# Where z enters the first branch, when the second branch is scaled, and how the forget rows are cleared

## The chip, the cores and the metric

The kernel runs on one core of one Trainium2 chip, as one launch. The metric is the device time of one execution in microseconds. A core has five engines that run their own instruction queues: TensorE (PE in the profile; its weight loads are shown as PEld), VectorE (DVE), ScalarE (ACT), GpSimd (POOL) and SyncE (SP), which here only issues transfers. Each engine runs its instructions in the order in which the program has them, and an instruction that waits holds all that stand behind it on its engine.

## The reference, cut to what matters

The block has two attention branches over the same normalised input, 512 tokens, 8 heads of 64 in each. The first ("fox", f) adds a forget term to its logits, the second ("moba", m) has rotated queries and keys and no forget term. Each branch's result is multiplied by a gate path made from z:

```
h = rms_norm(x, norm_g)
fq, fk, fv, fz, mq, mk, mv, mz, ga, gb, fl = split(h @ w_in)
c = cumsum(log_sigmoid(fl + b_f))
logits = q k^T * scale + c[query] - c[key]          # first branch, causal
y_fox = softmax(logits) @ v  * silu(fz)
y_moba = moba_attention(rope(q), rope(k), v) * silu(mz)
merged = sigmoid(ga + b0) * (y_fox @ w_fox) + sigmoid(gb + b1) * (y_moba @ w_moba)
out = x + merged @ w_out
```

## The kernel before, in words

Matrix products run as three products of a high and a low part each (`wh_`/`wl_`, `Gh`/`Gl`, `yh`/`yl`), which ACT and DVE make. Weights come in blocks of 512 KB, issued by SP into four buffers (`wr`).

Attention goes by four groups of four heads: first branch a and b, second branch a and b (`attn_group`, called from the loop over `plan`). A group has two pairs of heads. `Tr(pr)` transposes the pair's queries and keys on TensorE, and ACT and DVE make from them `QS`, `KH` and the low key part `KL`; half of `KH` is copied to the other 64 partitions by a transfer on ACT's queue. `Aa(h)` makes a head's logits (lines 558 and 559) and exponentials. `Bb(h)` transposes these, multiplies them by v and writes the head's half of the pair's tile y (line 638). `Yp(pr)` scales y by the inverse sums of the exponentials. Those go out through DRAM and come back spread over the partitions into the tile `rinv_bc` (`sums_out`, `sums_in`), which has one buffer in all but the last pair of the kernel; y of the first branch (`ypair`) has one buffer too.

In the first branch `Yp` also brings in z's gate `ZS` (lines 650 and 651): POOL multiplies it into the inverse sums, DVE multiplies y by that, and `gated` splits y into the two parts that the later product with `w_fox` reads. In the second branch `Yp` is one product on POOL (line 654); its gate comes later (line 806) and its split after that (`gated`, lines 508 and 509).

The four tiles `KLt[o][pr]` hold `KL` in 64 of their rows and, in the first branch, four forget rows in the other 64, brought in by SP (line 544); the remaining rows are zero from the start (`zero_kl`). The second branch uses the same tiles and needs the forget rows zero: `moba_begin` does this with four memsets of 32 rows on POOL, after the last logits of the first branch that read each tile. It is called between the second and third group.

POOL also does the powers, the scaling and the rotation of the queries and keys (lines 333, 335 and 365 to 371).

The program is written group by group, with projections of the next group laid between the parts (`inter`). The order on each engine is not the written one: the context is created with `schedule_with_timeline_sim=True`, a planner that simulates durations and orders each engine's instructions from that, by written order where several are ready. `attn_group` returns four lists: the head, the body, the tail, and the steps that go into the next group's body behind its first logits (`gate` in the loop).

Of the kernel before, what the change touches and what calls it, by code (L numbers as in the profile page):

```python
# [7 lines left out]
F32 = mybir.dt.float32  # L8
F32R = mybir.dt.float32r
AF = mybir.ActivationFunctionType  # L10
OP = mybir.AluOpType
# [18 lines left out]
def fox_moba_kernel(ctx: ExitStack, tc, xT, x, w_in, w_fl, w_fox, w_moba, w_out, cst, rope, out):  # L30


    nc = tc.nc
    V, A, G, T = nc.vector, nc.scalar, nc.gpsimd, nc.tensor
# [14 lines left out]
    def t2(tag, bufs, name, shape=(P, 512), dt=F32):  # L49
        pool = stage["pool"] if tag in ("qs", "pt", "pc", "ys") else sb  # L50
        return pool.tile(list(shape), dt, name=name, tag=tag, bufs=bufs)

    def pst(tag, bufs, name):
        return ps.tile([P, 512], F32, name=name, tag=tag, bufs=bufs)
# [4 lines left out]
    def tp(name):  # L59
        return pst("tp", 3, name)  # L60
# [347 lines left out]
    ZS = {}  # L408
# [81 lines left out]
    def moba_begin():  # L490
        for o in range(2):
            rows = slice(HD, HD + 32) if o == 0 else slice(0, 32)
            for tl in KLt[o]:
                G.memset(tl[rows, :].bitcast(F32), 0.0)


    Y = {}
# [7 lines left out]
    def gated(br, gp, y):  # L505
        yh = t2("y", 13, f"yh{br}{gp}", dt=F32R)
        yl = t2("y", 13, f"yl{br}{gp}", dt=F32R)
        A.activation(yh, y, AF.Copy)
        V.tensor_tensor(out=yl, in0=y, in1=yh.bitcast(F32), op=OP.subtract)
        Y[br, gp] = (yh, yl)  # L510

    def attn_group(br, half, gq, gk):
        fox = br == "f"
# [4 lines left out]
        def Tr(pr):  # L518
            def go():
                pq, pk = tp("p_qT"), tp("p_kT")  # L520
                for t in range(NT):
                    T.transpose(pq[:, t * P:(t + 1) * P], qn[:, t, pr * P:(pr + 1) * P], ident)  # L522
                for t in range(NT):
                    T.transpose(pk[:, t * P:(t + 1) * P], kn[:, t, pr * P:(pr + 1) * P], ident)
                for o in range(2):
                    h = 2 * pr + o
                    me, ot = (slice(0, HD), slice(HD, P)) if o == 0 else (slice(HD, P), slice(0, HD))
                    qs = t2("qs", 4, "QS", dt=F32R)
                    kh = t2("qs", 4, "KH", dt=F32R)
                    kl = KLt[o][pr]  # L530
                    A.activation(qs[me, :], pq[me, :], AF.Copy, scale=gq[me, :])  # L531
                    V.scalar_tensor_tensor(qs[ot, :], pq[me, :], gq[me, :], qs[me, :].bitcast(F32),  # L532
                                           op0=OP.mult, op1=OP.subtract)
                    A.activation(kh[me, :], pk[me, :], AF.Copy, scale=gk[me, :])
                    nc.scalar.dma_start(out=kh[ot, :].bitcast(F32), in_=kh[me, :].bitcast(F32))
                    V.scalar_tensor_tensor(kl[me, :], pk[me, :], gk[me, :], kh[me, :].bitcast(F32),
                                           op0=OP.mult, op1=OP.subtract)
                    q2 = qs
                    if fox:
                        q2 = Q2t[o]  # L540
                        lr = slice(HD, HD + 4) if o == 0 else slice(0, 4)
                        hh = hb + h
                        nc.sync.dma_start(out=q2[lr, :].bitcast(F32), in_=LR[hh:32:8, :].bitcast(F32))
                        nc.sync.dma_start(out=kl[lr, :].bitcast(F32), in_=LR[32 + hh:64:8, :].bitcast(F32))
                        nc.scalar.dma_start(out=q2[me, :].bitcast(F32), in_=qs[me, :].bitcast(F32))
                    st[h] = (qs, kh, kl, q2)
            return go

        def Aa(h):
            def go():  # L550
                qs, kh, kl, q2 = st[h]
                hh = hb + h
                pts = []
                for i in range(NT):
                    n = P * (i + 1)
                    lg = pst("lg", 2, "lg")
                    qt = slice(i * P, (i + 1) * P)
                    T.matmul(lg[:, :n], qs[:, qt], kh[:, :n], start=True, stop=False)  # L558
                    T.matmul(lg[:, :n], q2[:, qt], kl[:, :n], start=False, stop=True)  # L559
                    pt = stage["pool"].tile([P, n], F32, name=f"p{i}", tag=f"p{i}", bufs=2)  # L560
                    V.tensor_tensor_reduce(pt, lg[:, :n], mask[:, 512 - n:512], -0.125, 3.0e38,  # L561
                                           op0=OP.add, op1=OP.min, accum_out=mkn[:, hh, i:i + 1])
                    A.activation(pt, pt, AF.Exp, bias=mkn[:, hh, i:i + 1], scale=-1.0,  # L563
                                 accum_out=rs[:, hh, i:i + 1])
                    pts.append(pt)
                st[h] = pts
                if h % 2:
                    inverse_sums(h // 2)
                elif h:
                    sums_in(0)  # L570
            return go
# [4 lines left out]
        def inverse_sums(pr):  # L576
            h0 = hb + 2 * pr
            V.reciprocal(ri[:, h0:h0 + 2, :], rs[:, h0:h0 + 2, :])
# [16 lines left out]
        def Bb(h):  # L595
            def go():
                pts, vt = st[h], VT[f"{br}v{half}"]
                o = h % 2
                pv = pst("pv", 1, "pv")

                def blk(dst, i, j):
                    T.transpose(dst, pts[i][:, j * P:(j + 1) * P], ident)

                def spl(p, n):
                    tag, w, bufs = ("pt", 512, 4) if n == 512 else ("pc", 256, 2)
                    hi = t2(tag, bufs, "pth", (P, w), F32R)
                    lo = t2(tag, bufs, "ptl", (P, w), F32R)
                    A.activation(hi[:, :n], p[:, :n], AF.Copy)
                    V.tensor_tensor(out=lo[:, :n], in0=p[:, :n], in1=hi[:, :n].bitcast(F32), op=OP.subtract)
                    return hi, lo  # L610
                def pvm(j, hl, c0, n, start, stop):
                    T.matmul(pv[:, P * j:P * j + n], vt[:, j, h, :], hl[0][:, c0:c0 + n], start=start, stop=False)  # L612
                    T.matmul(pv[:, P * j:P * j + n], vt[:, j, h, :], hl[1][:, c0:c0 + n], start=False, stop=stop)  # L613
                pa = tp("p_a")
                for i in range(4):
                    blk(pa[:, i * P:(i + 1) * P], i, 0)
                pb = tp("p_b")
                for i in range(1, 4):
                    blk(pb[:, (i - 1) * P:i * P], i, 1)
                blk(pb[:, 384:512], 3, 3)  # L620
                ha = spl(pa, 512)
                hbb = spl(pb, 512)
                pc = tp("p_cc")
                for i in range(2, 4):
                    blk(pc[:, (i - 2) * P:(i - 1) * P], i, 2)
                hc = spl(pc, 256)
                pvm(0, ha, 0, 512, True, False)
                pvm(1, hbb, 0, 384, False, False)
                pvm(3, hbb, 384, 128, False, False)
                pvm(2, hc, 0, 256, False, True)  # L630
                pr = h // 2
                if o == 0:
                    st["y", pr] = t2("ys", 1, "ypair") if fox else t2("y", 13, f"ym{half}{pr}")
                y = st["y", pr]
                me, ot = (slice(0, HD), slice(HD, P)) if o == 0 else (slice(HD, P), slice(0, HD))
                sh = t2("uy", 1, "ysh")
                A.activation(sh[me, :], pv[ot, :], AF.Copy)
                V.tensor_tensor(out=y[me, :], in0=pv[me, :], in1=sh[me, :], op=OP.add)
                if o == 0:
                    sums_out(pr)  # L640
                elif pr:
                    sums_in(1)
            return go

        def Yp(pr):
            def go():
                y, rb = st["y", pr], st["r", pr]
                gp = 2 * (half == "b") + pr
                if fox:
                    G.tensor_tensor(out=rb, in0=ZS[br, gp], in1=rb, op=OP.mult)  # L650
                    V.tensor_tensor(out=y, in0=y, in1=rb, op=OP.mult)
                    gated(br, gp, y)
                else:
                    G.tensor_tensor(out=y, in0=y, in1=rb, op=OP.mult)
                    YM[gp] = y
            return go


        return ([Tr(0)], [Aa(0), Aa(1), Tr(1), Bb(0), Aa(2), Bb(1), Yp(0), Aa(3)], [Bb(2), Bb(3)], [Yp(1)])


    FS, MG = {}, {}
# [725 lines left out]
```

## Time and profile before

| | |
|---|---|
| median of 3 runs | 423.7 us (423.02 to 425.86) |
| profiled execution | 423.75 us |
| its span | 422.0 us |
| TensorE busy | 414.9 us |
| VectorE busy | 333.2 us |
| ScalarE busy | 273.6 us |
| GpSimd busy | 107.0 us |

The span is the time from the first to the last instruction of the profiled execution; the device time has 1.75 us more around it. Busy time counts an engine's instructions, not the waits and the issuing of transfers. The second branch's logits begin at about 167 us and the products with `w_fox` at about 247 us. The shares are means over the whole span; the stretches differ.

### The profile page before, as it was taken

How to read it: one execution, taken by the hardware profiler on the slowest of the kernel's cores; microseconds unless marked ns; L12 is line 12 of the kernel's file. 1: busy time of each engine (PE TensorE's matmuls, PEld its weight loads, DVE VectorE, ACT ScalarE, POOL GpSimd, SP SyncE). 2: the span in 40 equal slices, each digit the busy share in tenths (PEclk: the TensorE clock that was granted, in tenths of full speed). 3: DMA queues.
4: the chain of work that ended last, by engine and by line, in shares of the span. 5: the costliest groups of instructions: out<-in, count | busy, mean ns of one | idle time of the engine just before them, and what ended most of it. 6: DMA issues, size and time to landing. Idle time of an engine off the chain costs nothing.

```text
span 422.0 us, 7872 instructions
## 1 busy us (share of the span) xinstructions
PE 414.9 (98%) x2956; PEld 388.1 (92%) x2956; DVE 333.2 (79%) x571; ACT 273.6 (65%) x521; POOL 107.0 (25%) x127
## 2 busy tenths in 40 slices
PE   7999999999999999999999999999999999999996
PEld 6998899999999999999999998899999989988884
DVE  5669978797878997596977997637989675788982
ACT  4975437878769866796568876446847525685550
POOL 1049300252114690317600125120000020022240
PEclk9999999999999999999999999999999999999999
DMA  7981144654263662231048736623141726796394
GB/s 236 400 324 51 56 144 124 189 171 155 50 210 80 223 193 73 78 110 43 0 127 239 266 120 222 244 99 110 37 164 53 247 51 151 238 247 112 84 163 155
DMA packets 29703, 63.73 MB, mean 151 GB/s; under 512 B 3424, under 2 KB 10272, under 8 KB 29664
## 3 DMA queue, kind: packets, MB, share of 16 engines
q1 hardware_dynamic: 16880, 42.57, 30.3%
q0 software_dynamic: 3968, 9.44, 10.3%
q10 hardware_dynamic: 8816, 11.21, 9.1%
q8 instruction: 23, 0.38, 0.4%
q14 instruction: 16, 0.13, 0.1%
HBM read 52.56 MB, written 6.32 MB: 140 GB/s over the span
## 4 chain that ended last, share of the span: by engine, by line
PE 82%; DMA 6%; DVE 6%; ACT 2%; issue 1%; POOL 1%; SPq 1%; DVEq 0%; ACTq 0%
PE pb_GA L907 3%; PE pb_GB L907 3%; PE pb_GA L906 3%; PE pb_GB L904 3%; PE pb_GA L904 3%; PE pb_GB L906 3%; PE po L1093 3%; PE po L1091 3%; PE po L1092 3%; PE lg L559 2%; PE lg L558 2%; PE pv L613 2%; PE pv L612 2%; PE pGZ0a L771 2%; PE pGZ0b L771 2%; DMA x<-in_x_dram 2%
## 5 line engine op out<-in xcount | busy, mean ns | idle before, releaser
L333 POOL TENSOR_TENSOR ff<-ss,mh 128x8 f32<-128x8 f32 x16 | 27.8, 1741 | 60.6 <-DVE ss L331 51.8
L563 ACT ACTIVATE p<-p,negm 128x128 f32<-128x128 f32 (+1 forms) x64 | 35.7, 558 | 8.7 <-DVE negm L561 8.3
L561 DVE CUSTOM_DVE_ANT_0 p<-lg,mask 128x128 f32<-128x128 f32 (+1 forms) x64 | 30.2, 484 | 8.5 <-PE lg L559 8.2
L134 ACT ACTIVATE wh_GB<-wr_gb 128x1024 fp32r<-128x1024 f32 x14 | 14.6, 1058 | 13.4 <-PE pm L670 5.9
L136 DVE TENSOR_TENSOR wl_GA<-wr_ga,wh_GA 128x1024 fp32r<-128x1024 f32 x14 | 17.6, 1266 | 6.2 <-ACT wh_GA L134 6.2
L558 PE MATMUL lg<-KH,QS 128*128 128x128 f32 (+1 forms) x64 | 21.0, 333 | 0.2 <-DMA KH<-KH 0.2
L1053 ACT ACTIVATE wh_o<-wr_o 128x1024 fp32r<-128x1024 f32 x14 | 14.8, 1058 | 9.7 <-PE pb_GB L906 2.8
L974 POOL DMA_DIRECT2D uGB<-f x4 | 3.5, 869 | 69.4 <-issue 59.4
L136 DVE TENSOR_TENSOR wl_GB<-wr_gb,wh_GB 128x1024 fp32r<-128x1024 f32 x14 | 16.8, 1220 | 5.0 <-ACT wh_GB L134 5.0
L134 ACT ACTIVATE wh_GA<-wr_ga 128x1024 fp32r<-128x1024 f32 x14 | 14.6, 1059 | 9.2 <-PE pb_GA L906 5.9
L1054 DVE TENSOR_TENSOR wl_o<-wr_o,wh_o 128x1024 fp32r<-128x1024 f32 x14 | 16.9, 1218 | 2.4 <-ACT wh_o L1053 2.4
L532 DVE SCALAR_TENSOR_TENSOR QS<-p_qT,cs,QS 64x512 fp32r<-64x512 f32 x16 | 12.0, 750 | 4.1 <-ACT QS L531 3.7
L531 ACT ACTIVATE QS<-p_qT,cs 64x512 fp32r<-64x512 f32 x16 | 10.9, 680 | 4.1 <-PE p_qT L522 2.8
L904 PE MATMUL pb_GB<-Gh,wh_GB 128*128 128x256 f32 x48 | 13.5, 281 | 0.0
L904 PE MATMUL pb_GA<-Gh,wh_GA 128*128 128x256 f32 x48 | 13.5, 281 | 0.0
L906 PE MATMUL pb_GB<-Gl,wh_GB 128*128 128x256 f32 x48 | 13.5, 281 | 0.0
L906 PE MATMUL pb_GA<-Gl,wh_GA 128*128 128x256 f32 x48 | 13.5, 281 | 0.0
L907 PE MATMUL pb_GB<-Gh,wl_GB 128*128 128x256 f32 x48 | 13.5, 281 | 0.0
L907 PE MATMUL pb_GA<-Gh,wl_GA 128*128 128x256 f32 x48 | 13.5, 281 | 0.0
L669 PE MATMUL pf<-yhf,wh_wf 128*128 128x512 f32 x32 | 12.9, 402 | 0.0
L670 PE MATMUL pf<-ylf,wh_wf 128*128 128x512 f32 x32 | 12.7, 396 | 0.0
L558 PEld LDWEIGHTS lg<-KH,QS 128*128 128x128 f32 x64 | 12.1, 189 | 0.6 <-issue 0.3
(479 smaller groups left out, 1820.0 us busy)
## 6 DMA issues: line engine op xcount, KB each, us to landing
wr_ga<-in_w_in_dram SPq DMA_DIRECT2D x8, 512.0 KB
wr_gb<-in_w_in_dram SPq DMA_DIRECT2D x8, 512.0 KB
wr_o<-in_w_out_dram SPq DMA_DIRECT2D x8, 512.0 KB
xt<-in_xT_dram SPq DMA_DIRECT2D x8, 256.0 KB
x<-in_x_dram SPq DMA_DIRECT2D x8, 256.0 KB
KH<-KH ACTq DMA_DIRECT2D x16, 128.0 KB
s_dramh<-sum_h ACTq DMA_DIRECT2D x8, 256.0 KB
s_draml<-xt ACTq DMA_DIRECT2D x8, 256.0 KB
```

Of the source, the lines that this page charges most:

```text
L134: A.activation(hi[:, :, 0:n], src, AF.Copy)
L136: eng.tensor_tensor(out=lo[:, q, 0:n], in0=src[:, q], in1=hi[:, q, 0:n].bitcast(F32), op=OP.subtract)
L333: G.tensor_tensor(out=f2, in0=ss.rearrange("p t h -> p (t h)"), in1=mh, op=OP.pow)
L558: T.matmul(lg[:, :n], qs[:, qt], kh[:, :n], start=True, stop=False)
L561: V.tensor_tensor_reduce(pt, lg[:, :n], mask[:, 512 - n:512], -0.125, 3.0e38, op0=OP.add, op1=OP.min, accum_out=mkn[:, hh, i:i + 1])
L563: A.activation(pt, pt, AF.Exp, bias=mkn[:, hh, i:i + 1], scale=-1.0, accum_out=rs[:, hh, i:i + 1])
L771: T.matmul(o, x, y, start=(new and h == 0 and k == 0 and i == 0), stop=(k == 3 and i == 2), skip_group_check=True)
L904: T.matmul(o, hi[:, k, cc], lh, start=(n < 3 and c == 0 and k == 0), stop=False, skip_group_check=True)
L906: T.matmul(o, hi[:, k, cc], ll, start=False, stop=False, skip_group_check=True)
L907: T.matmul(o, lo[:, k, cc], lh, start=False, stop=(k == 3), skip_group_check=True)
L1053: A.activation(wide(hi), wide(R[key, c]), AF.Copy)
L1054: V.tensor_tensor(out=wide(lo), in0=wide(R[key, c]), in1=wide(hi).bitcast(F32), op=OP.subtract)
```

## The change

Three edits. In the first branch POOL multiplies z's gate into y itself, and DVE then multiplies by the inverse sums. In the first group of the second branch the first scaling, `Yp(0)`, goes from before the group's last logits into the late list, so that both scalings are written in the next group's body. And the forget rows are cleared by four transfers on SP, which copy four zero rows of the same tile over them, in place of four memsets on POOL.

```diff
     def moba_begin():
         for o in range(2):
             rows = slice(HD, HD + 32) if o == 0 else slice(0, 32)
+            a = rows.start
             for tl in KLt[o]:
-                G.memset(tl[rows, :].bitcast(F32), 0.0)
+                nc.sync.dma_start(out=tl[a:a + 4, :].bitcast(F32), in_=tl[a + 4:a + 8, :].bitcast(F32))
...
                 if fox:
-                    G.tensor_tensor(out=rb, in0=ZS[br, gp], in1=rb, op=OP.mult)
+                    G.tensor_tensor(out=y, in0=y, in1=ZS[br, gp], op=OP.mult)
                     V.tensor_tensor(out=y, in0=y, in1=rb, op=OP.mult)
                     gated(br, gp, y)
...
-        return ([Tr(0)], [Aa(0), Aa(1), Tr(1), Bb(0), Aa(2), Bb(1), Yp(0), Aa(3)], [Bb(2), Bb(3)], [Yp(1)])
+        early, late = ([Yp(0)], [Yp(1)]) if fox or half == "b" else ([], [Yp(0), Yp(1)])
+        return ([Tr(0)], [Aa(0), Aa(1), Tr(1), Bb(0), Aa(2), Bb(1)] + early + [Aa(3)], [Bb(2), Bb(3)], late)
```

## Rows read from the trace of the kernel before

**Rows 1.** The page, busy us (share of the span) and instructions of each engine.

```profile
PE 414.9 (98%) x2956; PEld 388.1 (92%) x2956; DVE 333.2 (79%) x571; ACT 273.6 (65%) x521; POOL 107.0 (25%) x127
```

**Rows 2.** Busy time by stretch: from:to, length, engines, granted clock, transfers' share.

```profile
core 0: us, PE busy (x) PEld busy (x) DVE busy (x) ACT busy (x) POOL busy (x), PEclk, DMA share, GB/s
...
141.00:160.00 19.00, 18.66 (x152) 18.14 (x151) 16.86 (x34) 13.06 (x30) 17.31 (x21) 1.00 0.58 183
```

**Rows 3.** TensorE's waits, 60 to 280 us: total us, times, longest.

```profile
PE p_qT L522 <- POOL qn_mqa L371: 0.3, 1, 0.3
PE lg L558 <- DMA KH<-KH: 0.2, 1, 0.2
```

**Rows 4.** Timeline of TensorE: start us, us, line, operation, tiles, [idle before].

```profile
153.12 0.29 PE L305 MATMUL pj_mva<-wh_mva,Gh 128*128 128x256 f32 x1
153.24 0.28 PE L306 MATMUL pj_mva<-wl_mva,Gh 128*128 128x256 f32 x1
153.87 0.44 PE L522 MATMUL p_qT<-ident,qn_mqa 128*128 128x128 f32 x2 [0.34 <-POOL qn_mqa L371]
...
160.57 0.38 PE L522 MATMUL p_qT<-ident,qn_mqa 128*128 128x128 f32 x2
...
166.92 0.28 PE L559 MATMUL lg<-KL,QS 128*128 128x128 f32 x1
```

**Rows 5.** The chain that ended last, between 143 and 160: start us, us, what.

```profile
147.60 1.30 POOL rinv_bc L650
...
153.36 0.46 POOL qn_mqa L371
```

**Rows 6.** Timeline of POOL, columns as in rows 4; last row by line 494.

```profile
121.44 0.52 POOL L494 MEMSET KL<- 32x512 f32 x1 [14.65 <-issue]
...
144.42 0.52 POOL L494 MEMSET KL<- 32x512 f32 x1
...
154.38 1.65 POOL L333 TENSOR_TENSOR ff<-ss,mh 128x8 f32<-128x8 f32 x1
...
158.66 0.46 POOL L371 TENSOR_TENSOR qn_mqa<-ra,rb 128x128 f32<-128x128 f32 x1
...
202.50 2.33 POOL L654 TENSOR_TENSOR yma<-yma,rinv_bc 128x512 f32<-128x512 f32 x1 [3.88 <-DVE yma L638]
...
L494 POOL MEMSET KL<- x4: 514/518/520, 121.4 to 153.8; 32x512 f32 x4
```

**Rows 7.** Timeline of DVE, 147 to 165 us.

```profile
147.61 2.38 DVE L136 TENSOR_TENSOR wl_mkb<-wr_mkb,wh_mkb 128x1024 fp32r<-128x1024 f32 x1 [0.50 <-ACT wh_mkb L134]
...
153.03 0.69 DVE L638 TENSOR_TENSOR ypair<-pv,ysh 64x512 f32<-64x512 f32 x1
...
155.42 0.69 DVE L651 TENSOR_TENSOR ypair<-ypair,rinv_bc 128x512 f32<-128x512 f32 x1
...
164.68 1.23 DVE L136 TENSOR_TENSOR wl_mqb<-wr_mqb,wh_mqb 128x1024 fp32r<-128x1024 f32 x1
```

**Rows 8.** Tile KL (ns: min/median/max), SP's and ACT's timelines, the chain's first load.

```profile
L544 SPq DMA_DIRECT2D KL<-LR x8: 577/577/607, 68.7 to 102.5; - x8
...
135.65 1.57 SPq L210 DMA_DIRECT2D wr_mqb<-in_w_in_dram  x2
...
163.58 1.06 ACT L134 ACTIVATE wh_mqb<-wr_mqb 128x1024 fp32r<-128x1024 f32 x1
...
8.94 7.00 DMA wr_fka<-in_w_in_dram
```

**Rows 9.** The chain at 214 us, and TensorE's row that follows it.

```profile
214.66 4.17 DMA KH<-KH
...
218.97 0.30 PE L558 MATMUL lg<-KH,QS 128*128 128x128 f32 x1 [0.17 <-DMA KH<-KH]
```

**Rows 10.** First reader of the first branch's y; split of the second's (tile yma).

```profile
247.26 0.39 PE L669 MATMUL pf<-yhf,wh_wf 128*128 128x512 f32 x1
...
L508 ACT ACTIVATE yhm<-yma x2: 628/630/632, 275.4 to 302.6; 128x512 fp32r<-128x512 f32 x2
```

## The prediction, made before the change was run

> **What bounds the kernel now.** I read the page's busy shares first: TensorE (PE) is busy for 98% of the span, VectorE (DVE) for 79%, ScalarE (ACT) for 65%, GpSimd (POOL) for 25% [rows 1]. So a change to POOL's work is worth only what it takes from, or adds to, TensorE's pauses. The view of busy time by stretch says where POOL is nevertheless tight: between 141 and 160 us it works 17.31 of 19.00 us, and that is also a stretch in which TensorE falls short, by 0.34 us, at full granted clock [rows 2]. Third, TensorE's waits between 60 and 280 us, the whole part in which changed instructions run: there are two, 0.3 us for POOL's rotated queries `qn_mqa` (line 371) and 0.2 us for a copy of key halves, `KH` [rows 3].
>
> The busy bar hides a part of a pause, because the end of a matmul is modelled. Starts are better: 153.12 to 153.24 is the usual 0.12 us for 256 columns, and then the next matmul, the transpose of `qn_mqa`, starts at 153.87, 0.63 us later [rows 4]. So this wait costs 0.63 - 0.12 = 0.51 us. The chain of waits shows what stood before that transpose: POOL's z product from 147.60 to 148.90, four rotation and scaling steps, and the last of them at 153.36 [rows 5]. The z product (line 650) has nothing to do with the transpose; it merely stands ahead in POOL's queue. The second wait starts from a `KH` copy of 4.17 us and shows 0.17 us idle [rows 9].
>
> **Part 1, z is multiplied into y.** No instruction is added or removed: four POOL products of 128x512, each with two full operands, stay four, and so do the four DVE products. Old: POOL waits for the inverse sums, new: for y, the pair's weighted values (line 638). In the second group of the first branch the second half of y starts at 153.03 for some 0.69 us, so is there at 153.72, while the old product ran at 147.60 [rows 5, 7]. It can therefore not run ahead of the first `qn_mqa` chain any more: 1.30 us leave that chain, against 0.51 us of wait. Gain: 0.51 us if the transposes keep their place in TensorE's order, 0 if the planner moves them up with their inputs and meets the same slow POOL steps again. I take 0.51, as the row at hand has 1.30 us to give and the memset below 0.52 more.
>
> What is late next: the product now wants POOL at 153.72, and POOL starts the second `qn_mqa` chain at 154.38, ending at 158.66 + 0.46 = 159.12; TensorE transposes that half at 160.57, so there are 1.45 us of room for a product of 1.30 [rows 4, 6]. It fits, barely. On DVE the scaling of y stood at 155.42 [rows 7]; it now waits for POOL, and behind it in DVE's queue stand the evacuations of the value projection. That is the slow case below. The results, the first branch's products split into two parts, are first read by TensorE at 247.26 [rows 10]: lateness of the values themselves costs nothing.
>
> **Part 2, forget rows.** Removed from POOL: four memsets, 0.518 us each in the median, 2.07 us together, of which one (144.42) lies in the chain that TensorE waits for, and one only held POOL with nothing else to do (14.65 us before 121.44) [rows 6]. On the chain that is part of the 0.51 already counted, so nothing is added. New on SyncE's queue (SP): four transfers of four rows. The nearest issue is the transfer of the forget rows themselves, the same four rows of the same tile: 0.577 us on SP [rows 8], so 4 x 0.577 = 2.3 us of SP. Its landing has no row; bounds are near nothing and the 4.17 us of a `KH` copy inside SBUF [rows 9], which is 16 times as many rows, and I take the upper one. The last memset began at 153.8 [rows 6]; a transfer from there would land by 158.0, and the second branch first multiplies with such a tile at 166.92 [rows 4]: 8.9 us of cover. If that cover were gone, each late clear would cost up to its 4.17 us.
>
> Behind a clear that must wait, SP holds weight loads. Worst order: the last tile's clear ahead of the load of `wr_mqb`, issued at 135.65. The clear waits for the last forget product, no later than 153.8; the load (7.00 us for a like one in the chain) would land near 161.4 with the 0.577 us of the clear, and its split starts at 163.58 [rows 6, 8]. So even this costs nothing, with 2.2 us left. Price 0, bounds 0 and 2.3 us (all four issues uncovered).
>
> **Part 3, the second branch's first scaling later.** The product at 202.50 (2.33 us, after 3.88 us in which POOL was held for y) leaves its place [rows 6]. The inverse sums have one buffer there, so the load for the next pair waits for it; the split of these values starts only at 275.4 [rows 10], so I price it at 0. It could free the `KH` wait, 0.17 us [rows 9]; but that chain starts from TensorE's own transposes, so I take 0. Bounds: 0.17 us gained to nothing.
>
> **Sum.** 423.75 us, the profiled execution (span 422.0, so 1.75 us around it), - 0.51 + 0 + 0 = 423.24. The median of the three runs is 423.7, 0.05 below the profiled one, so I forecast 423.2. Run to run the kernel moved from 423.02 to 425.86.
>
> **A rule weighed.** At 147.61 DVE's split of `wr_mkb`, two operands in SBUF, took 2.38 us; the same shape at 164.68 took 1.23 [rows 7]. POOL's z product ran at the same moment [rows 5]. So one overlap cost DVE 1.15 us. The Trainium skill, SBUF — State Buffer, section SBUF: two separate sides, says that GpSimd shares a port pair with VectorE as a lock, and that a VectorE instruction with two SBUF inputs fully blocks until GpSimd's reading instruction is over. The trace agrees with that here; by the rule the four products could block DVE for up to 4 x 1.30 = 5.2 us (an estimate from that page and the row), and the sum would lie that much nearer the slow case. I leave DVE's loss at one overlap, as now, since the number of products stays four.
>
> **Rivals.**
>
> *The wait is kept* (0.27). The program's order on each engine comes from a planner that simulates durations; the memset that held POOL 14.65 us shows that it misjudges them [rows 6]. It may move the transposes up as soon as it thinks the inputs are there. Then a 0.5 us wait stands there again: 423.7, 423.2 to 424.2.
>
> *DVE is held for POOL: slower* (0.20). Place: 153.7 to 160.4. If POOL runs the product after the second `qn_mqa` chain, it ends at 159.12 + 1.30 = 160.42, and DVE, standing at its scaling since 155.42, is held 5.0 us [rows 6, 7]. TensorE fills a projection unit of 24 matmuls in 24 x 0.12 = 2.9 us [rows 4], and the projections have two accumulator buffers, so it can hide about one unit: 5.0 - 2.9 = 2.1 us lost, 423.7 + 2.1 = 425.8. With the lock of the rows above on top (1.15) it is 427.0. It decides as soon as DVE's hold passes 2.9 us. Against it: the planner knows of POOL's queue and would put DVE's scaling later.
>
> *SP's clears are in the way* (0.05): 423.7 + 2.3 = 426.0.
>
> *The lock decides* (0.04), the page's rule as a mechanism of this kernel: three more overlaps of 1.15 us on DVE, 3.45 us, in stretches where TensorE waits for DVE: 423.7 + 3.45 = 427.2, and over 1% slower with any wait beside it.
>
> *The change moves nothing it names*: that the order on all engines stays but for the swapped operands is part of the second case.
>
> **How the numbers follow.** Forecast 0.42 (422.6 to 423.8), wait kept 0.27, DVE held 0.20, SP 0.05, lock 0.04, and 0.02 for a gain that I can't see. Below, both waits and nothing new would give 423.7 - 0.51 - 0.17 = 423.0; with the 0.7 us by which the fastest run lies below the median, 422.3, and I set 422.1. Above, DVE held is 425.8, and I set 426.2, which leaves the lock and the worse half of DVE held outside. What a measurement of this kernel can tell from no change is 1%, 4.2 us: below 419.5 or above 427.9. TensorE's waits in the changed part sum to 0.68 us, so faster than that is next to excluded: 0.02. Slower takes DVE held at its worst and the lock: 0.06. Within: 0.92.
>
> **What would show it.** Right: no TensorE wait for `qn_mqa`, POOL's z product behind y at each of four places, POOL under 17 us busy between 141 and 160, memsets gone, and SP's clears well before the second branch's first logits. Wrong: a TensorE pause of over 1 us between 150 and 170 that goes back to DVE's scaling and from there to POOL; or DVE steps of 2 us beside the z products; or a weight split that waits for a load behind a clear. A pause anywhere that traces to none of these would mean that the new plan itself, not the three edits, decides.

## The result: slower by 1.1%, by a change of order in a stage that no edit touches

| | before | after |
|---|---|---|
| median | 423.64 us (422.99 to 425.86, 6 runs) | 428.64 us (426.69 to 430.54, 6 runs) |
| ratio after to before | | 1.0112, interval 1.0075 to 1.0149 |
| profiled execution, span | 423.75 us, 422.0 us | 426.69 us, 424.9 us |

The forecast was 423.2 us within 422.1 to 426.2. The time lies outside of it, on the side that had a chance of 0.06. The profiled execution is the shortest of the six, so its trace holds 2.9 us of the 5.0 by which the medians differ; the rest is looked for in three more traces below.

The page of the changed kernel, the row that answers to [rows 1]:

```profile
PE 415.3 (98%) x2956; PEld 388.4 (91%) x2956; DVE 330.0 (78%) x571; ACT 272.9 (64%) x521; POOL 105.1 (25%) x123
```

Every engine but TensorE has less to do, DVE by 3.2 us. So nothing became costlier by its busy time; the loss must be in waits. TensorE's waits from 60 to 420 us, in total, number and longest:

```profile
PE pb_GB L906 <- ACT wh_GB L134: 1.9, 1, 1.9
PE lg L559 <- DMA KH<-KH: 0.9, 2, 0.6
```

Beside [rows 3], the wait for `qn_mqa` is gone, the one for `KH` has grown, and there is a new one of 1.9 us in a stage that no edit touches: the gates (`GA`, `GB`), whose first matmuls stood at 277 us before. TensorE's timeline shows the places (start, us, line, operation, tiles, idle before):

```profile
153.01 0.39 PE L560 MATMUL lg<-KL,Q 128*128 128x512 f32 x1
153.24 0.38 PE L523 MATMUL p_qT<-ident,qn_mqa 128*128 128x128 f32 x2
...
218.14 0.28 PE L613 MATMUL pv<-pth,v_mva 128*128 128x256 f32 x1
219.01 0.30 PE L559 MATMUL lg<-KH,QS 128*128 128x128 f32 x1 [0.59 <-DMA KH<-KH]
...
309.04 0.28 PE L908 MATMUL pb_GA<-Gl,wh_GA 128*128 128x256 f32 x1
311.20 0.39 PE L906 MATMUL pb_GB<-Gh,wh_GB 128*128 128x256 f32 x1 [1.89 <-ACT wh_GB L134]
311.43 0.28 PE L908 MATMUL pb_GB<-Gl,wh_GB 128*128 128x256 f32 x1
311.54 0.28 PE L909 MATMUL pb_GA<-Gh,wl_GA 128*128 128x256 f32 x1
```

At 153 the transposes of `qn_mqa` follow without a gap, where [rows 4] had 0.63 us between two starts. At 218 there are 0.87 us between starts, at 309 there are 2.16. Two matmuls of `GB` stand there in the middle of a unit of `GA`: 19 more of that unit follow them, from 311.54 to 313.68. In the kernel before, the same two matmuls of `GB` stand between two units of `GA`:

```profile
311.19 0.28 PE L904 MATMUL pb_GB<-Gh,wh_GB 128*128 128x256 f32 x1
311.31 0.28 PE L906 MATMUL pb_GB<-Gl,wh_GB 128*128 128x256 f32 x1
311.43 0.28 PE L904 MATMUL pb_GA<-S3h,wh_GA 128*128 128x256 f32 x1
```

Counted in the traces, 48 matmuls of `GA` come behind them before and 70 in the changed kernel. So the planner also moved these two up in TensorE's order, by 22 matmuls or 22 x 0.12 = 2.6 us.

The chain of waits goes back from that pause (start, us, what):

```profile
304.93 1.23 DVE wl_GA L136
306.18 3.81 DMA wr_gb<-in_w_in_dram
...
310.09 1.07 ACT wh_GB L134
...
311.20 0.39 PE pb_GB L906
```

DVE's low part of a weight block frees the buffer, SP issues the load of the next block (`wr_gb`), it lands 3.8 us later, ACT splits it, TensorE starts. In the kernel before that load was issued earlier, by SP's timeline of before:

```profile
303.56 0.33 SPq L871 DMA_DIRECT2D wr_gb<-in_w_in_dram  x1
```

That left room there. ACT's timeline of before has the split of that block:

```profile
308.41 1.06 ACT L134 ACTIVATE wh_GB<-wr_gb 128x1024 fp32r<-128x1024 f32 x1 [1.23 <-PE pb_GA L906]
```

The high part is ready at 309.47 there, and TensorE reads it at 311.19. The load is 2.6 us later now, because DVE is. DVE's timeline of the kernel before, in the stretch where that begins:

```profile
291.95 0.68 DVE L917 TENSOR_TENSOR uGA<-pb_GA,e_GA 128x512 f32<-128x512 f32 x1
292.55 1.21 DVE L866 TENSOR_TENSOR wr_ga<-wr_ga,wr_ga 128x1024 f32<-128x1024 f32 x1
294.59 0.69 DVE L917 TENSOR_TENSOR uGA<-pb_GA,e_GA 128x512 f32<-128x512 f32 x1 [0.82 <-PE pb_GA L907]
295.37 1.22 DVE L953 TENSOR_TENSOR f<-uGA,f 128x1024 f32<-128x1024 f32 x1
```

And of the changed kernel (the first three rows are of the edited stage, used further down):

```profile
148.70 1.22 DVE L136 TENSOR_TENSOR wl_mkb<-wr_mkb,wh_mkb 128x1024 fp32r<-128x1024 f32 x1
...
152.56 0.69 DVE L639 TENSOR_TENSOR ypair<-pv,ysh 64x512 f32<-64x512 f32 x1
...
154.66 0.69 DVE L652 TENSOR_TENSOR ypair<-ypair,rinv_bc 128x512 f32<-128x512 f32 x1
...
292.28 0.68 DVE L919 TENSOR_TENSOR uGA<-pb_GA,e_GA 128x512 f32<-128x512 f32 x1
294.91 0.69 DVE L919 TENSOR_TENSOR uGA<-pb_GA,e_GA 128x512 f32<-128x512 f32 x1 [1.95 <-PE pb_GA L909]
295.70 1.23 DVE L955 TENSOR_TENSOR f<-uGA,f 128x1024 f32<-128x1024 f32 x1
296.85 1.22 DVE L868 TENSOR_TENSOR wr_ga<-wr_ga,wr_ga 128x1024 f32<-128x1024 f32 x1
299.25 2.36 DVE L136 TENSOR_TENSOR wl_GA<-wr_ga,wh_GA 128x1024 fp32r<-128x1024 f32 x2 [1.19 <-ACT wh_GA L134]
```

Before, the second weight subtraction (L866) stood ahead of the sum (L917) that must wait for TensorE, and filled that wait: 0.82 us idle. Now it stands behind the sum and behind a product: DVE idles 1.95 us, and then 1.19 us more for ACT's split. That split needs the late subtraction, which ends at 298.07, and it also stands behind an exponential on ACT that waits for TensorE and ends at 298.10; before, it stood ahead of that exponential. Either would have held it. ACT's row in the changed kernel:

```profile
297.50 0.60 ACT L916 ACTIVATE e_GA<-pb_GA 128x512 f32<-128x512 f32 x1 [0.95 <-PE pb_GA L909]
```

From 299.25 to 312.5 DVE runs without a gap and can't catch up. 1.95 + 1.19 - 0.82 = 2.3 us, near the 2.6 by which the load is late.

The pause has two parts, then. The high part of `GB`'s first block is ready at 311.15 instead of 309.47, 1.7 us later; and TensorE comes to it at 309.16 instead of 311.19, 2.0 us earlier. Together 3.7 us, less the 1.7 us of room before: 2.0 us. By an estimate from these rows the late load alone would have cost nothing here (with TensorE's order of before it would be wanted 2.6 us later, at 311.8), and the new place in TensorE's order alone some 0.9 us (309.47 against 308.6). No run has one without the other, so this division is not shown by experiment.

### The profile page after: what moved, and what is told of

Same layout as the page of the kernel before. It is cut to its first block, busy times and chain, and to the rows that moved or that the text cites. A ratio compares the mean times of both kernels' runs of the same rounds, so it can differ in the third digit from the quotient of the medians.

```text
span 424.9 us, 7866 instructions
## 1 busy us (share of the span) xinstructions
PE 415.3 (98%) x2956; PEld 388.4 (91%) x2956; DVE 330.0 (78%) x571; ACT 272.9 (64%) x521; POOL 105.1 (25%) x123
## 3 DMA queue, kind: packets, MB, share of 16 engines
q0 software_dynamic: 3968, 9.44, 10.3%
## 4 chain that ended last, share of the span: by engine, by line
PE 76%; DMA 11%; DVE 7%; ACT 2%; issue 2%; SPq 1%; DVEq 0%; ACTq 0%
PE pb_GB L906 3%; PE pb_GB L909 3%; PE pb_GB L908 3%; PE po L1095 3%; PE po L1093 3%; PE po L1094 3%; PE pb_GA L909 2%; PE pb_GA L906 2%; PE pb_GA L908 2%; PE pv L614 2%; PE lg L559 2%; PE lg L560 2%; PE pv L613 2%; DMA x<-in_x_dram 2%; PE pf L672 2%
## 5 line engine op out<-in xcount | busy, mean ns | idle before, releaser
L333 POOL TENSOR_TENSOR ff<-ss,mh 128x8 f32<-128x8 f32 x16 | 29.1, 1825 | 96.0 <-DVE ss L331 95.4
L610 DVE TENSOR_TENSOR ptl<-p_a,pth 128x512 fp32r<-128x512 f32 x16 | 11.0, 686 | 4.6 <-ACT pth L609 4.5
L610 DVE TENSOR_TENSOR ptl<-p_b,pth 128x512 fp32r<-128x512 f32 x16 | 11.0, 685 | 4.3 <-ACT pth L609 4.2
L638 ACT ACTIVATE ysh<-pv 64x512 f32<-64x512 f32 x16 | 9.5, 594 | 6.8 <-PE pv L614 6.7
L609 ACT ACTIVATE pth<-p_b 128x512 fp32r<-128x512 f32 x16 | 9.5, 594 | 6.6 <-PE p_b L603 6.6
```

Of the source, the lines that this page charges most:

```text
L333: G.tensor_tensor(out=f2, in0=ss.rearrange("p t h -> p (t h)"), in1=mh, op=OP.pow)
```

## Theories, and a sum by stage

My theory (A in the expectations): the z edit costs nothing where it stands, but it makes the planner put the gates' steps in another order, and that order is the loss. The first rival: each z product that was changed costs something at its place, on POOL or DVE (C in e1 to e4, in the form that the prediction gave it, DVE held; B in e5 to e8, in general). The second: the other two edits carry part of it (B in e1 to e4 names SP's clears). The last three expectations name two theories of their own, C and D, for another question.

For all traces I summed, over TensorE's matmuls, the time from one start to the next less the usual interval of that shape (its 10th percentile in the trace). The sum by stage, in us, tells where TensorE falls short:

| trace | span | median, ratio to before | 0 to 20 | 140 to 200 (edited stage) | 200 to 250 (`KH`) | 285 to 320 (gates) |
|---|---|---|---|---|---|---|
| before | 422.0 |  | 3.7 | 8.8 | 7.2 | 0.8 |
| after | 424.9 | 428.64, 1.0112 | 3.7 | 8.1 | 8.1 | 3.2 |
| e1 z only | 425.9 | 428.17, 1.0105 | 4.3 | 8.2 | 8.6 | 2.8 |
| e2 without z | 422.5 | 424.19, 1.0007 | 5.1 | 8.2 | 7.1 | 0.8 |
| e3 gates ordered | 426.1 | 429.68, 1.0137 | 3.9 | 8.1 | 7.9 | 4.5 |
| e4 before, gates late | 426.5 | 428.14, 1.0114 | 3.6 | 8.7 | 8.2 | 4.3 |
| e5 one z product | 426.7 | 427.29, 1.0095 | 5.4 | 8.3 | 8.6 | 2.8 |
| e6 three z products | 421.5 | 423.49, 0.9997 | 3.8 | 8.3 | 7.5 | 0.8 |
| e7 all edits, two z | 421.4 | 423.89, 1.0002 | 3.9 | 8.7 | 7.2 | 0.8 |
| e8 gates sum held | 425.4 | 428.89, 1.0138 | 4.2 | 8.1 | 8.3 | 3.2 |

The gates column falls into two groups, 0.8 and 2.8 or more, and the medians fall into the same two. TensorE's order falls into them too: 48 matmuls of `GA` stand behind `GB`'s first two in before, e2, e6 and e7, and 70 in all others. The column of the edited stage, where the z products of the second group run, does not follow the medians: it is lower in after, e1 and e5 than in before.

## The experiments

**e1, the z edit alone.** The kernel before with one line changed:

```diff
-                    G.tensor_tensor(out=rb, in0=ZS[br, gp], in1=rb, op=OP.mult)
+                    G.tensor_tensor(out=y, in0=y, in1=ZS[br, gp], op=OP.mult)
```

> Only the first edit (z multiplied into y on POOL); scaling order and memsets as before. Theory A (the z edit makes the planner put the gates' weight subtractions and splits at about 297 us behind the products that wait for TensorE, so that a weight load of the next gate group starts some 2.6 us late and TensorE pauses about 2 us near 309 us): that pause is there, 426.5 to 429.5. Theory B (SyncE's clears hold the loads): no pause, 423.7 plus or minus 0.6. Theory C (the slow case of the prediction, DVE held at its scaling of y): the loss stands between 150 and 170 us, 426 to 428, with a TensorE pause there.

428.17 us (427.61 to 428.58), ratio 1.0105 [1.0089, 1.0121]. The whole loss, with the pause near 310, so the other two edits have nothing left to explain. Theory C, DVE held at its scaling, is out as well: TensorE falls short by less from 140 to 200 us than before.

**e2, the other two edits without it.** The kernel before with the clears by SP and the later scaling, z as before.

> The other two edits without the first one: later first scaling in the second branch, forget rows cleared by SyncE's transfers. Theory A: the order of the gates' splits is that of the kernel before, so no pause near 309 us and 423.7 plus or minus 0.8. Theory B: the wr_gb load late, pause near 309, 426.5 to 429. Theory C: 423.7.

424.19 us, ratio 1.0007 [0.999, 1.0023]. Both edits together are free, as parts 2 and 3 of the forecast said. The waits for `qn_mqa` and `KH` are gone in this trace and the time is no shorter.

**e3, the gates put in order by constraints.** The changed kernel; two sums' groups of `GA0` are bound behind steps of the next product's preparation:

```diff
-                evac(n)
+                if name == "GA0" and n > 4:
+                    with tc.issue_after(MARK["sub" if n == 5 else "hi"]):
+                        evac(n)
+                else:
+                    evac(n)
```

> The changed kernel with one more constraint: in the gates, the first gate group's last sums and sigmoids must be issued behind the second group's weight subtractions (DVE) and splits (ACT). No work is added or removed. Theory A: the pause near 309 us goes (1.9 us in the trace of after), and with it 2 to 5 us: 423.8 to 425.5; what remains above 423.7 are two waits for KH copies, about 1.3 us against 0.3 before. Theories B and C: as the changed kernel, 427 to 430.

429.68 us, ratio 1.0137 [1.0109, 1.0165]: no cure. Its ACT timeline shows a new wait of the same sort:

```profile
296.81 2.01 ACT L134 ACTIVATE wh_GA<-wr_ga 128x1024 fp32r<-128x1024 f32 x2 [6.55 <-DVE wr_ga L869]
```

The constraint moved one sum, and the planner put another sum, which waited 2.58 us for TensorE, ahead of the subtraction. The run decides nothing between the theories; it shows that this constraint did not bring the order back.

**e4, the kernel before with its gates disturbed.** No edit of the change; only the preparation written ahead of the sixth unit of `GA0` is put behind that unit:

```diff
+                    if behind:
+                        u()
+                        with tc.issue_after(last_on(mybir.EngineType.DVE)):
+                            pump(i)
+                        return
```

> The kernel before, none of the three edits, but at one unit of the first gate group the weight preparation is traced behind the unit and issued behind its last DVE instruction, which gives the gates about the order that the changed kernel has (subtractions and splits behind the products). Theory A: a pause near 309 us of 1.5 to 2.5 us, 425.5 to 429. Theories B and C: 423.7 plus or minus 0.6.

428.14 us, ratio 1.0114 [1.0077, 1.0152]. TensorE's waits:

```profile
PE pb_GB L904 <- ACT wh_GB L134: 1.7, 1, 1.7
PE pb_GA L904 <- DVE uGA L917: 0.9, 1, 0.9
```

The loss of the change, with none of the change in it: an order of the gates can cost that much by itself. It is not quite the order of the changed kernel: the first two matmuls of `GB` stand 22 places earlier here too, but a second wait (for `uGA`) is added, and the gates column is 4.3 against 3.2. That it is the order in the changed kernel needed e5 to e7.

**e5, one of the four z products.** The new product only in the first pair of the second group (`gp` 2).

```diff
-                    G.tensor_tensor(out=rb, in0=ZS[br, gp], in1=rb, op=OP.mult)
+                    if gp in (2,):
+                        G.tensor_tensor(out=y, in0=y, in1=ZS[br, gp], op=OP.mult)
+                    else:
+                        G.tensor_tensor(out=rb, in0=ZS[br, gp], in1=rb, op=OP.mult)
```

> The kernel before with a single one of the four z products changed, that of the first pair of the second group of the first branch (gp 2): POOL multiplies z into y there and into the inverse sums in the other three. In this program the last 100 steps of ScalarE (the gates and what follows) stand in the order that they have in the changed kernel. Theory A (the z edit costs through the order of the gates stage, 130 us later, in which a weight subtraction stands behind a sum that TensorE has not delivered): one product is enough for the whole loss, 427 to 429 us, TensorE pausing for wh_GB near 309 by 1.5 to 2.5 us. Theory B (each changed product costs something where it stands, on POOL or DVE): a quarter of 4.1 to 5.0 us, so 424.7 to 425.3, and no pause at 309 beyond a quarter of that.

427.29 us, ratio 1.0095 [1.0064, 1.0126], and the same DVE rows as in the changed kernel, 2.06 us later:

```profile
296.97 0.69 DVE L920 TENSOR_TENSOR uGA<-pb_GA,e_GA 128x512 f32<-128x512 f32 x1 [1.95 <-PE pb_GA L910]
297.77 1.23 DVE L956 TENSOR_TENSOR f<-uGA,f 128x1024 f32<-128x1024 f32 x1
298.91 1.22 DVE L869 TENSOR_TENSOR wr_ga<-wr_ga,wr_ga 128x1024 f32<-128x1024 f32 x1
```

One product of 1.3 us, moved by some microseconds, carries nearly all of the loss. An equal price at each place would have given a quarter. That this one place alone has a price is the rival left, since every slow run but e4 has this product changed. Two things speak against it: TensorE falls short by 8.3 us from 140 to 200, where this product runs, against 8.8 before, and e4 has the loss without it.

**e6, the other three.** The same edit with `gp in (0, 1, 3)`.

> The kernel before with the other three z products changed (gp 0, 1 and 3) and that of gp 2 as before. In this program the last 100 steps of ScalarE stand as in the kernel before, but for one normalisation of two that is two places later. Theory A: no loss, 423.2 to 425.0 us, no pause at 309. Theory B: three quarters of the loss, 426.7 to 427.5. If it is between, both hold in part, and the pauses tell how much.

423.49 us, ratio 0.9997 [0.9976, 1.0019]. Three quarters of the edit cost nothing, and DVE's rows stand as before:

```profile
291.64 1.22 DVE L869 TENSOR_TENSOR wr_ga<-wr_ga,wr_ga 128x1024 f32<-128x1024 f32 x1
293.68 0.69 DVE L920 TENSOR_TENSOR uGA<-pb_GA,e_GA 128x512 f32<-128x512 f32 x1 [0.82 <-PE pb_GA L910]
```

Subtraction ahead of the sum, 0.82 us idle: with that order, no loss. An equal price at each place is out. TensorE's only listed wait from 60 to 420 us in this trace is this one:

```profile
PE pGZ0a L774 <- DMA Gl<-s_draml: 0.2, 1, 0.2
```

**e7, all three edits with two of four z products** (`gp in (0, 3)`).

> The changed kernel with all three edits, but the z edit at two of its four products only (gp 0 and 3). The last 100 steps of ScalarE stand as in the kernel before. Theory A: 422.8 to 424.5 us, no pause at 309, and the wait for qn_mqa gone. Theory B: half of the loss, 425.8 to 426.5. A third view, that the three edits together make DVE or SP late somewhere that the single ones do not: over 426 with a pause that is at neither 218 nor 309.

423.89 us, ratio 1.0002 [0.9985, 1.0019]: no loss, and no third mechanism from the edits together. The product of `gp` 2 is not among the two, so this run too has the gates' order of before. One point of the expectation missed: the wait for `qn_mqa`, said to be gone, is there (0.3 us) and costs nothing that can be told.

**e8, a second try to restore the gates' order**, the changed kernel with one sum's group held behind the last subtraction (the edit of e3 with `n == 5` alone).

> The changed kernel, whole, with one constraint more, other than the earlier one: the evacuation of the sixth unit of the first gates product may not be issued before the last weight subtraction that the next gates product's second unit needs. By that the subtraction stands ahead of the sum again on DVE, and ScalarE makes both weight parts before the next exponential, as before. Theory A: the weight load of wr_gb is issued 2 us or more earlier than at 306.2, the pause near 309 is gone, and of the loss there remain the longer waits for KH near 218 and 239 (about 0.9 us more than before): 424.5 to 426.5. Theory B: stays at 428 to 429. It could also miss, as the earlier constraint did, if another order among the gates' steps turns up; then a pause of over 1 us stands between 290 and 320 at another place.

428.89 us, ratio 1.0138 [1.0108, 1.0169]: missed, in the way that its expectation named last. DVE:

```profile
295.46 0.69 DVE L924 TENSOR_TENSOR uGA<-pb_GA,e_GA 128x512 f32<-128x512 f32 x1 [2.58 <-PE pb_GA L914]
296.07 1.22 DVE L869 TENSOR_TENSOR wr_ga<-wr_ga,wr_ga 128x1024 f32<-128x1024 f32 x1
```

The held sum went behind the subtraction, and the sum of another unit, which waits for TensorE, came in front of it. A version of the whole change with the gates' order of before was not found.

**e9 to e11, the changed kernel three times more**, for the 2 us between its profiled execution and its median.

> The changed kernel once more, for another trace. Open is the size: its profiled execution took 426.69 us, 2.9 more than the kernel before, while its median is 428.64; five of its six executions are longer than the profiled one, four of these at a mean granted clock of 0.994 or 0.995 against 1.0. Theory C: in those executions the clock falls for some us after the pause near 309, by half, and that is the rest of the loss: a mean of 0.995 over 425 us is 2.1 us of lost clock, and an execution at 0.995 takes 428.5 to 430.5 us with the fall in the stretch from 305 to 325. Theory D: the clock falls elsewhere or by nothing, and the longer executions are longer by longer waits (the load of wr_gb, KH): then the pauses of this trace sum to 2 us more than those of the first.

> The same kernel and question as the look before it. Theory C: if the mean clock is 1.0, 426.5 to 428 us and the pauses of the first trace; if it is 0.994 to 0.996, 428.5 to 430.5 us with the fall behind the pause near 309. Theory D: the time does not go with the clock.

> The same kernel and question as the two looks before it. Theory C: if the mean clock is 1.0, 426.5 to 428 us and the pauses of the first trace; if it is 0.994 to 0.996, 428.5 to 430.5 us with the fall behind the pause near 309. Theory D: the time does not go with the clock.

429.47, 428.69 and 428.08 us. All three have the pause in the gates, 2.0 to 2.1 us longer than the usual interval. Beside it each has something else. In e9 it is the `KH` copies, by TensorE's waits:

```profile
PE lg L559 <- DMA KH<-KH: 3.2, 2, 1.7
```

and by the chain's row of the second of them, here behind the row of the same copy in the first trace:

```profile
234.56 4.85 DMA KH<-KH
...
235.96 6.16 DMA KH<-KH
```

In e10 it is TensorE's clock. Busy time by stretch as in [rows 2], then the granted clock:

```profile
308.00:312.00 4.00, 2.14 (x18) 1.94 (x17) 4.00 (x6) 2.74 (x5) 0.00 (x0) 1.00 0.86 260
312.00:316.00 4.00, 4.00 (x23) 4.00 (x22) 3.44 (x4) 0.11 (x1) 0.00 (x0) 0.57 0.68 225
316.00:320.00 4.00, 4.00 (x36) 4.00 (x35) 2.33 (x3) 1.25 (x2) 0.00 (x0) 1.00 0.07 29
```

Behind the pause, in which TensorE did nothing for 2.0 us, it runs for some 3.4 us at the lower level (1.2 GHz) and does 23 matmuls where the next 4 us hold 36: 13 x 0.12 = 1.6 us lost. In e11 the clock is full, the wait for `qn_mqa` is back (0.3 us), and there is another for a softmax maximum (0.3 us). So C holds in e10 and D in e9; e11, at full clock, took 428.08 where C allowed 428, and leans to D. Neither holds alone. The executions without a trace point to the clock as well: of the nine on record of the changed kernel, five (e10 among them) have a mean granted clock of 0.994 or 0.995 and took 428.54 to 430.54 us; the four at 0.998 or 1.0 took 426.69 to 429.47, 1.2 us less on average. Where the clock fell in those without a trace is not known.

Over the four traces of the changed kernel, against the one of before, the shortfall of TensorE is on average 4.63 us more: gates 2.68 (3.17, 3.20, 4.61 and 3.15, less 0.85), `KH` 1.42 (8.09, 10.25, 8.14 and 8.04, less 7.21), the start of the kernel 0.36, which moves between runs of any kernel here (3.6 to 5.4), the rest 0.17. That is the difference of the medians within half a microsecond. That the longer `KH` waits come from the new order too was not tried by itself. Speaking for it: in e2, e6 and e7 that column is 7.1 to 7.5, and in the traces of after, e1, e3, e5 and e8 it is 7.9 to 10.3. e4, with 8.2, has its waits there for other transfers, so the column is no pure measure. About 1.4 of the 4.6 us, then, has a place but no shown cause.

## Why the prediction was wrong

**The step that failed** is the first paragraph's choice of stretch: "TensorE's waits between 60 and 280 us, the whole part in which changed instructions run". All prices, and all rivals, were of places where an edited instruction stands, and what lies behind 280 us was carried over unchanged. The prediction knew of the planner: it gave "the wait is kept" 0.27 on that ground, and ended with "the new plan itself, not the three edits, decides". It gave that last case no place, no price and no chance, and it was the one that came: 2.7 us of TensorE's shortfall lie in the gates at 285 to 320 us, and 1.4 us, of open cause, from 200 to 250, where the `KH` waits are.

What could have been read: in the kernel before, DVE stands without a gap of note from 294.59 to 311.08, ACT has the high part of `GB`'s first block ready at 309.47, and TensorE wants it at 311.19, so 1.7 us of room for a load that DVE's order times. A new order there had a price, and any edit that shifts the planner's simulated times could bring one. Which edits do can't be told from the trace (e5 does, e6 does not). It can be told from the new program itself before it runs: the expectations of e5 to e7 compare ScalarE's last 100 steps with those of the two kernels, and all three came out. Without that, the order could have been taken as unknown, with a share of the chance on the slow side well above 0.06.

**Part 1, the wait for `qn_mqa` goes, 0.51 us gained.** It went, and the z product left the chain as forecast. POOL's timeline of the changed kernel:

```profile
148.76 1.34 POOL L367 TENSOR_TENSOR rb<-qn_mqa,tab_mq 128x64 f32<-128x64 f32 x1
...
150.46 1.32 POOL L371 TENSOR_TENSOR qn_mqa<-ra,rb 128x128 f32<-128x128 f32 x1
153.33 1.29 POOL L651 TENSOR_TENSOR ypair<-ypair,zs_fzb 128x512 f32<-128x512 f32 x1 [1.56 <-DVE ypair L639]
154.58 1.65 POOL L333 TENSOR_TENSOR ff<-ss,mh 128x8 f32<-128x8 f32 x1
...
158.82 0.46 POOL L371 TENSOR_TENSOR qn_mqa<-ra,rb 128x128 f32<-128x128 f32 x1
...
205.05 1.30 POOL L655 TENSOR_TENSOR yma<-yma,rinv_bc 128x512 f32<-128x512 f32 x1 [5.84 <-DVE yma L639]
```

The first chain ends at 151.78 instead of 153.82 [rows 5]. The z product stands behind y, at 153.33 where 153.72 was expected, and the second chain ends at 159.28 where the forecast left room until 160.57. The gain came at its place: from 140 to 200 us TensorE falls short by 8.6 to 8.8 us in the traces that have the wait (before, e4, e7, e11) and by 8.1 to 8.3 in those without it (after, e1, e2, e3, e5, e6, e8, e9, e10). That is 0.3 to 0.7 us, near the 0.51. But the z product's leaving is neither needed nor enough for it. In e2 the product is still ahead of the chain, at 147.72, and there is no wait; in e11 it stands behind the chain, at 154.93, and the wait is back, in the same program as the changed kernel. Whether the gain reaches the whole time isn't shown: 0.51 us is a ratio of 0.9988, just outside the interval of e2 and inside that of e6.

**DVE held for POOL (0.20)** did not happen. DVE's scaling (L652) runs at 154.66, right behind the product; the planner put it behind other work of DVE, as the argument against that rival said.

**The lock (0.04)** did not decide. In the changed kernel the two-operand split at 148.70 took 1.22 us; its like of before had taken 2.38 [rows 7]. This time POOL lost: its small rotation step at 148.76 took 1.34 us, the next like it (150.06) 0.32. The Trainium skill, SBUF — State Buffer, section SBUF: two separate sides, says that whichever of the two starts first has the pair and the other blocks; the trace agrees, DVE started 0.06 us earlier here. DVE's busy time in that stretch fell from 16.86 [rows 2] to 14.51 us, and TensorE was busy for all of its 19.00 us.

**SP's clears (0.05)** cost nothing. SP's timeline:

```profile
122.24 0.58 SPq L495 DMA_DIRECT2D KL<-KL  x1
...
134.96 1.69 SPq L210 DMA_DIRECT2D wr_mqb<-in_w_in_dram  x2
...
153.44 0.60 SPq L495 DMA_DIRECT2D KL<-KL  x1
```

They take the 0.58 us of the row that they were priced by [rows 8], and the weight load stands 0.7 us earlier than before. **The later scaling** runs at 205.05, and none of the waits of TensorE listed above is for it.

## What to carry to other kernels

Where a planner orders the instructions, the price of an edit has two parts: what it does at its place, and what the new plan does to stages that have no room; the second can be the larger, and it isn't proportional to the edit (one of four products cost 4 us, the other three nothing). Before a forecast, look for the stage where an engine runs without a gap and its order times a load, and give a changed order there a price and a chance. After a result that nobody can explain at the edit, compare the order of the untouched stages first, and undo the edit piece by piece: pieces that keep the order tell the edit's own cost.

## What the runs showed of the hardware

The same pause of about 2.1 us was followed by some 3.4 us at the lower clock in one of four traces of one program, and by the full clock in three. The Trainium skill, TensorE: Matmul & The Clock Gate, Part 1, says that the gate follows how busy the array has been of late and that its effect varies between runs of one kernel; the traces agree, with 1.6 us in one trace and none in the others.

The mean granted clock was 0.994 or 0.995 in five of the nine executions, so the fall may be more frequent than the four traces show.

The `KH` copy that starts near 235 us, 128 KB as the trace counts it, took 4.85 us in the first trace of the changed kernel, 4.73 in e10, 4.67 in e11 and 6.16 in e9: one copy of one program, 1.3 us and more apart from one execution to another.
